# Two weight sums and one lo half of the FFN's fast product, made by adding DMA writes

## The chip, the cores and the metric

The kernel runs on one core of a Trainium2 chip. The engines of that core are TensorE (PE, with its weight loads PEld), VectorE (DVE), ScalarE (ACT), GpSimd (POOL) and SyncE (SP), which here only issues DMAs. The metric is the device time of one execution in microseconds (us). Before the change it is 2390.55 us, the median of three runs (2388.98 to 2391.84).

## The reference

One inference step of a 2-layer trunk for 512 prompt positions and 32 sample positions, which the kernel treats as 544 columns. All data is float32. Each layer has two gated feed-forward blocks (FFN) around a mixer and a memory attention:

```python
def _swiglu(x, wg, wu, wd):
    return (jax.nn.silu(x @ wg) * (x @ wu)) @ wd

x = x + 0.5 * _swiglu(_rmsnorm(x, n[0]), f1_wg[l], f1_wu[l], f1_wd[l])   # D_MODEL 1024, D_FF 2816
...
x = x + 0.5 * _swiglu(_rmsnorm(x, n[3]), f2_wg[l], f2_wu[l], f2_wd[l])
```

So there are four FFNs, f1 and f2 of either layer. The change is in the products `x @ wg` and `x @ wu`.

## The kernel before

**Split precision.** Every float32 operand is split in a hi half (a float32r copy, made by ACT) and a lo half (what is left, `source - hi`, made by VectorE). A product of two operands is three matmuls, hi·hi, hi·lo and lo·hi (`TERMS`, line 263). A weight tile is thus loaded raw, copied by ACT into `[:, 0]` and its remainder written by VectorE into `[:, 1]`.

**A fast 2x2 product.** For the gate and up projections a pair of 128-column blocks of the weights, both halves of the contraction and both halves of the columns of x are taken as 2x2 blocks, and a scheme with seven block products in place of eight is used. One such unit of work is called a pair, `P` (line 469). It reads 16 weight blocks of 128x128 per pair from `raw`, in four groups of four: blocks 0 to 3, 4 to 7, 8 to 11 and 12 to 15. Its weight operands are

- `al`: blocks 0 to 7 as they are (a12 and a11), used by products 2 and 1. `al_h` is the hi half (ACT), `al_l` the lo half (VectorE).
- `be`: two sums, `sb` = (blocks 4 to 7, blocks 8 to 11) each plus blocks 12 to 15 (`be_s`, VectorE), then hi (`be_h`, ACT) and lo (`be_l`, VectorE); products 7 and 5.
- `ga`: two further sums (`ga_s`, VectorE, into the tile `sg`), hi (`ga_h`) and lo (`ga_l`); products 6 and 3.
- `de`: blocks 8 to 11 as they are, `de_h` and `de_l`; product 4.

Each of the seven products is 12 matmuls of 272 columns (`prod`, line 390): four blocks of the contraction, and for each the three terms, the lo half of the weight being in the third.

**Order.** The order on every engine is the order in the program. For each FFN there are three parts: part 0 with 4 up pairs, after ordinary gate units (`gate`) have been computed for the same columns; part 1 with 8 pairs and part 2 with 6, gate and up in turn. That makes 18 pairs in an FFN and 72 in all. After each part a down projection (`dps`) follows. `run` (line 478) lays out seven steps for each pair: p1, p5, p4 of the pair before, p6, p2, p3, p7. Between them stands what the next pair, `N`, needs: `al_h` ahead of p4, `al_l` ahead of p6, `be_s` ahead of p2, `be_h` and `ga_s` ahead of p3, `be_l` and `ga_h` ahead of p7; `ga_l` stands ahead of the pair's own p1. The second pair of a part has no pair before it whose p4 is open when its `al_h` is made. The first pair of a part is prepared by `prelude` (line 474), one unit of TensorE work (48 matmuls) ahead of its p1.

**Loads and buffers.** Raw weights come in blocks of 1 MB through two buffers (`rawp`); `release` (line 153) issues the next block on SP when the last reader of a block is done, which for a pair is `de_l`. Split weights `al` and `be` take three buffers (`wcp`); `sb`, `sg`, `ga`, `de` and the hidden activations take 13 (`dp`). In the product stages POOL has no work.

Of the kernel before, what the change touches and what calls it, by code (L numbers as in the profile page):

```python
# [7 lines left out]
F32 = mybir.dt.float32  # L8
F32R = mybir.dt.float32r
AF = mybir.ActivationFunctionType  # L10
ALU = mybir.AluOpType
# [18 lines left out]
class Unit:  # L30
    def __init__(self, blk, k0, nk, c0, nc):
        self.blk, self.k0, self.nk, self.c0, self.nc = blk, k0, nk, c0, nc
        self.on_pool = self.late = self.raw = self.manual = False


class Block:
    def __init__(self, ap):
        self.ap = ap
        self.nk, self.nc = ap.shape[1], ap.shape[2]
        self.left = 0  # L40
        self.tile = None

    def unit(self, k0, nk, c0, nc):
        self.left += 1
# [4 lines left out]
def trunk_kernel(ctx, tc, I, O):  # L49
    nc = tc.nc  # L50
    pe, act, dve, pool, sp = nc.tensor, nc.scalar, nc.vector, nc.gpsimd, nc.sync
    keep = ctx.enter_context(tc.tile_pool(name="keep", bufs=1))
    up = ctx.enter_context(tc.tile_pool(name="up", bufs=49))
# [9 lines left out]
    def nm(s):  # L63
        cnt[0] += 1
        return f"{s}{cnt[0]}"
# [4 lines left out]
    def D(shape, dt=F32, n="d"):  # L70
        return dp.tile(shape, dt, tag="d", name=nm(n))
# [13 lines left out]
    def tt(e, out, a, b, op):  # L85
        e.tensor_tensor(out=out, in0=a, in1=b, op=op)  # L86
# [4 lines left out]
    def actv(out, a, f, **kw):  # L91
        act.activation(out=out, in_=a, func=f, **kw)  # L92
# [13 lines left out]
    def step(fn, *units, la=3, ahead=None):  # L106
        steps.append((fn, units, la, ahead))
# [7 lines left out]
    def flush():  # L115
        l, later[:] = list(later), []
        for f in l:
            f()
        for w in waiting:
            w[0] -= 1  # L120
        due = [w for w in waiting if w[0] <= 0]
        waiting[:] = [w for w in waiting if w[0] > 0]
        for w in due:
            w[1]()

    def emit_steps():
        order = []
        for _, us, _, _ in steps:
            order.extend(us)
        blks = []  # L130
        for u in order:
            if u.blk not in blks[-3:]:
                blks.append(u.blk)
        st = {"dma": 0, "conv": 0}

        def issue(part=0):
            if part:
                b = blks[0]
                h = b.nk // 2
                sp.dma_start(out=b.tile[:, h:], in_=b.ap[:, h:])  # L140
                return
            if st["dma"] >= len(blks):
                return
            b = blks[st["dma"]]
            st["dma"] += 1
            b.tile = rawp.tile([128, b.nk, b.nc], F32, tag="raw", name=nm("raw"))
            if st["dma"] == 1:
                h = b.nk // 2
                sp.dma_start(out=b.tile[:, 0:h], in_=b.ap[:, 0:h])
            else:  # L150
                sp.dma_start(out=b.tile, in_=b.ap)

        def release(u):
            u.blk.left -= 1
            if u.blk.left == 0:
                issue()

        def conv(defer=None):
            u = order[st["conv"]]
            st["conv"] += 1  # L160
            if u.manual:
                return
            w = wcp.tile([128, 2, u.nk, u.nc], F32R, tag="wc", name=nm("wc"))
            src = u.blk.tile[:, u.k0:u.k0 + u.nk, u.c0:u.c0 + u.nc]
            actv(w[:, 0], src, AF.Copy)
            u.tile = w

            def low():
                tt(pool if u.on_pool else dve, w[:, 1], src, w[:, 0].bitcast(F32), ALU.subtract)
                if not u.raw:  # L170
                    release(u)
            if defer is None or not u.late:
                low()
            else:
                defer.append(low)

        S["release"] = release
        startup(C_NORM, issue, conv)
        used = 0
        for fn, us, la, ahead in steps:  # L180
            used += len(us)
            flush()
            post = []
            while ahead is not None and st["conv"] < min(len(order), used + ahead):
                conv()
            while us and st["conv"] < min(len(order), used - len(us) + la):
                conv(post)
            fn(*us)
            for f in post:
                f()  # L190
            for u in us:
                if u.raw:
                    release(u)
        while later or waiting:
            flush()
# [95 lines left out]
    def ffn(which, l, next_g, tail=None):  # L291
# [53 lines left out]
        def low(lo, src, hi):  # L345
            tt(dve, lo, src, hi.bitcast(F32), ALU.subtract)

        def al_h(P):
            P.al = wcp.tile([128, 2, 8, 128], F32R, tag="wc", name=nm("wc"))
            actv(P.al[:, 0], P.blk.tile[:, 0:8], AF.Copy)  # L350

        def al_l(P):
            low(P.al[:, 1], P.blk.tile[:, 0:8], P.al[:, 0])

        def be_s(P):
            r = P.blk.tile.rearrange("p (z k) n -> p z (k n)", k=4)
            P.sb = D([128, 8, 128], n="sb")
            tt(dve, P.sb.rearrange("p (z k) n -> p z (k n)", k=4), r[:, 3:4].to_broadcast([128, 2, 512]), r[:, 1:3], ALU.add)

        def be_h(P):  # L360
            P.be = wcp.tile([128, 2, 8, 128], F32R, tag="wc", name=nm("wc"))
# [5 lines left out]

        def ga_s(P):
            r = P.blk.tile
            P.sg = D([128, 8, 128], n="sg")  # L370
            tt(dve, P.sg[:, 0:4], P.sb[:, 4:8], r[:, 4:8], ALU.add)
            tt(dve, P.sg[:, 4:8], P.sg[:, 0:4], r[:, 0:4], ALU.add)

        def ga_h(P):
            P.ga = D([128, 8, 128], F32R, n="ga"), D([128, 8, 128], F32R, n="ga")
            actv(P.ga[0], P.sg, AF.Copy)

        def ga_l(P):
            low(P.ga[1], P.sg, P.ga[0])
            P.sg = None  # L380

        def de_h(P):
            P.de = D([128, 2, 4, 128], F32R, n="de")
            actv(P.de[:, 0], P.blk.tile[:, 8:12], AF.Copy)

        def de_l(P):
            low(P.de[:, 1], P.blk.tile[:, 8:12], P.de[:, 0])
            S["release"](P)

        def prod(P, i, bank, first=False):  # L390
            w = {1: lambda p: P.al[:, p, 4:8], 2: lambda p: P.al[:, p, 0:4], 7: lambda p: P.be[:, p, 0:4], 5: lambda p: P.be[:, p, 4:8],
                 6: lambda p: P.ga[p][:, 0:4], 3: lambda p: P.ga[p][:, 4:8], 4: lambda p: P.de[:, p]}[i]
            for kp in range(4):
                for j, (p, xx) in enumerate(TERMS):
                    pe.matmul(out=bank[:, 0:HT], lhsT=w(p)[:, kp], rhs=XF[i, kp][xx], start=first and kp == 0 and j == 0,  # L395
                              stop=kp == 3 and j == 2, skip_group_check=not first)
# [24 lines left out]
        def p6(P):  # L421
            prod(P, 6, P.A)
            actv(P.s[:, 0], P.A[:, 0:HT], AF.Copy)

        def p2(P):
            B = PS("wB")
            prod(P, 2, B, True)
            P.al = None
            tt(dve, P.q[:, 0], B[:, 0:HT], P.q[:, 0], ALU.add)
            if P.up:  # L430
                g = G[P.p, 0]
                tt(dve, g[:, 0], P.q[:, 0], g[:, 0], ALU.mult)
                P.q = None
            else:
                actv(P.q[:, 0], P.q[:, 0], AF.Silu)
# [31 lines left out]
            P.A = None  # L467

        def pair(w, p, up):
            P = Block(w[p]).unit(0, 16, 0, 128)  # L470
            P.manual, P.up, P.p = True, up, p
            return P

        def prelude(P):
            for f in (al_h, be_s, ga_s, be_h, al_l, be_l, ga_h):
                f(P)

        def run(items):
            for i, P in enumerate(items):
                N = items[i + 1] if i + 1 < len(items) else None  # L480
                Q = items[i - 1] if i else None

                def nx(*fs, N=N):
                    for f in fs:
                        if N:
                            f(N)
                step(lambda _, P=P: (ga_l(P), p1(P)), P, la=1)
                step(lambda P=P: p5(P))
                step(lambda Q=Q, nx=nx: (nx(al_h), Q and p4(Q)), ahead=None if N else 1)
                step(lambda P=P, nx=nx: (de_h(P), nx(al_l), p6(P)))  # L490
                step(lambda P=P, nx=nx: (de_l(P), nx(be_s), p2(P)))
                step(lambda P=P, nx=nx: (nx(be_h, ga_s), p3(P)), ahead=None if N else 2)
                step(lambda P=P, nx=nx: (nx(be_l, ga_h), p7(P)))

        ks_of = lambda p0, np: [(k, 2 * p0 + k) for k in range(2 * np)]
        for part, (p0, np) in enumerate(((0, 4), (4, 4), (8, 3))):
            prs = range(p0, p0 + np)
            if part == 0:
                items = [pair(wu, p, True) for p in prs]
                for p in prs:  # L500
                    blk = Block(wg[p])
# [32 lines left out]
            for n2 in range(4):  # L534
                blk = Block(wd[n2])
                us += [blk.unit(0, 2 * np, i * 128, 128) for i in range(2)]
            a, b = ks[:-2], ks[-2:]
# [1485 lines left out]
```

## Time and profile before

| What | us |
|---|---|
| median of three runs | 2390.55 |
| lowest and highest of them | 2388.98, 2391.84 |
| the profiled execution | 2391.14 |
| its span | 2389.3 |
| its granted TensorE clock, mean | 0.996 of full |

The profile is of one execution. In its page "busy" is the time in which an engine had an instruction running; a group's row has the line, the engine, the tiles (out<-in), the count, then busy time and mean duration, then the idle time of the engine just before these instructions and what ended it. Most operations go through helpers (`tt` at line 86, `actv` at line 92, `mm` at line 95, the products at line 395), so the tiles' names tell them apart. The timeline has one row for each instruction or run of equal instructions: start and duration in us. A DMA's row has its size and the median time from issue to landing.

### The profile page before, as it was taken

Reading aid. Unit: us, or ns where it says so; the run is one execution under the profiler, and the core shown is the slowest. Engines: PE = TensorE matmul, PEld = TensorE weight load, DVE = VectorE, ACT = ScalarE, POOL = GpSimd, SP = SyncE. Lnnn points to the kernel's source line nnn. Section 1 sums busy time; section 2 is a strip of 40 time slices with the busy share of each in tenths; the row PEclk is TensorE's granted clock in tenths of the full one; section 3 lists DMA queues with packets and bytes.
Section 4 is the critical chain, followed back from the end, with each engine's and each line's share of the span. In section 5 each row is a group of like instructions: output and inputs, shape, how many; then the busy total and the mean of one; then the engine's idle time right before and its main releaser. Section 6 shows DMA issues by size and latency. Waiting matters only on the chain.

```text
span 2389.3 us, 46376 instructions
## 1 busy us (share of the span) xinstructions
PE 2349.7 (98%) x20030; PEld 2285.2 (96%) x20030; DVE 1570.2 (66%) x2443; ACT 1067.9 (45%) x1783; POOL 232.6 (10%) x243
## 2 busy tenths in 40 slices
PE   8999999998999999999999999999999999999998
PEld 8999999998889989999999999999999989999998
DVE  8758475668656655867666876747445656948484
ACT  6435255724545344534434543525443444525254
POOL 0000001244221103000000000000313002000001
PEclk9999999999999999999999999999999999999999
DMA  4222234223445471232322222322322552223222
GB/s 146 89 89 97 85 107 137 89 81 117 146 153 186 160 287 71 71 108 87 107 89 90 88 106 80 115 72 93 123 92 88 203 221 76 84 89 107 106 85 78
DMA packets 69197, 268.69 MB, mean 112 GB/s; under 512 B 15072, under 2 KB 22240, under 8 KB 45952
## 3 DMA queue, kind: packets, MB, share of 16 engines
q1 hardware_dynamic: 55264, 243.72, 29.1%
q10 hardware_dynamic: 13728, 22.01, 2.7%
q8 instruction: 157, 2.57, 0.4%
q14 instruction: 48, 0.39, 0.0%
HBM read 253.47 MB, written 12.23 MB: 111 GB/s over the span
## 4 chain that ended last, share of the span: by engine, by line
PE 86%; DVE 9%; ACT 2%; issue 1%; POOL 1%; DMA 0%; SPq 0%; ACTq 0%; DVEq 0%; POOLq 0%
PE dps L95 21%; PE wA L395 18%; PE wC L395 9%; PE wo L95 8%; PE wB L395 4%; PE vp L95 4%; PE q L95 4%; PE pA L95 2%; PE gps L95 2%; PE kp L95 2%; PE pB L95 2%; DVE wc L86 1%; DVE xf L86 1%; PE up L95 1%; PE sc L95 1%
## 5 line engine op out<-in xcount | busy, mean ns | idle before, releaser
L86 DVE TENSOR_TENSOR wc<-raw,wc 128x1024 fp32r<-128x1024 f32 (+1 forms) x306 | 381.9, 1253 | 250.5 <-ACT wc L92 249.6
L95 PE MATMUL dps<-hid,wc 128*128 128x272 f32 x4224 | 534.9, 288 | 0.6 <-DVE wc L86 0.6
L95 PEld LDWEIGHTS dps<-hid,wc 128*128 128x128 f32 x4224 | 531.5, 188 | 1.3 <-DVE wc L86 1.2
L92 ACT ACTIVATE wc<-raw 128x1024 fp32r<-128x1024 f32 (+1 forms) x322 | 331.0, 1032 | 249.9 <-PE dps L95 201.3
L89 DVE SCALAR_TENSOR_TENSOR x<-dps,x 128x272 f32<-128x272 f32 x192 | 75.7, 434 | 212.1 <-PE dps L95 212.1
L95 PE MATMUL gps<-xd,wc 128*128 128x272 f32 x1344 | 177.2, 291 | 7.5 <-ACT xd L92 6.8
L95 PEld LDWEIGHTS gps<-xd,wc 128*128 128x128 f32 x1344 | 172.8, 190 | 8.3 <-ACT xd L92 6.8
L86 POOL TENSOR_TENSOR ss<-ss,sq 128x544 f32<-128x544 f32 x47 | 65.4, 1392 | 1181.2 <-ACT sq L92 1172.5
L395 PE MATMUL wA<-xb,wc 128*128 128x272 f32 x864 | 122.2, 290 | 7.8 <-DVE wc L86 7.8
L92 ACT ACTIVATE wc<-sb 128x1024 fp32r<-128x1024 f32 x72 | 76.0, 1056 | 112.8 <-DVE sb L86 87.4
L395 PE MATMUL wC<-xf,wc 128*128 128x272 f32 x864 | 124.2, 292 | 0.4 <-DVE wc L86 0.4
L395 PEld LDWEIGHTS wA<-xb,wc 128*128 128x128 f32 x864 | 113.9, 190 | 8.9 <-DVE wc L86 8.7
L395 PE MATMUL wA<-xf,ga 128*128 128x272 f32 x864 | 120.3, 288 | 0.2
L395 PE MATMUL wA<-xf,wc 128*128 128x272 f32 x864 | 120.1, 288 | 0.0
L395 PE MATMUL wA<-xf,de 128*128 128x272 f32 x864 | 120.1, 288 | 0.0
L395 PE MATMUL wC<-xf,ga 128*128 128x272 f32 x864 | 120.0, 288 | 0.0
L395 PE MATMUL wB<-xf,wc 128*128 128x272 f32 x864 | 119.9, 288 | 0.0
L395 PEld LDWEIGHTS wC<-xf,wc 128*128 128x128 f32 x864 | 114.9, 190 | 2.7 <-DVE wc L86 1.3
L395 PEld LDWEIGHTS wA<-xf,ga 128*128 128x128 f32 x864 | 112.9, 188 | 0.9 <-ACT q L92 0.9
L395 PEld LDWEIGHTS wA<-xf,wc 128*128 128x128 f32 x864 | 112.9, 188 | 0.0
L395 PEld LDWEIGHTS wC<-xf,ga 128*128 128x128 f32 x864 | 112.9, 188 | 0.0
L395 PEld LDWEIGHTS wB<-xf,wc 128*128 128x128 f32 x864 | 112.8, 188 | 0.0
(366 smaller groups left out, 4428.0 us busy)
## 6 DMA issues: line engine op xcount, KB each, us to landing
raw<-in_f_wu_dram SPq DMA_DIRECT2D x44, 1024.0 KB, 4.7
raw<-in_f_wg_dram SPq DMA_DIRECT2D x43, 1024.0 KB, 4.8
raw<-in_f_wda_dram SPq DMA_DIRECT2D x16, 1024.0 KB, 4.8
raw<-in_f_wdb_dram SPq DMA_DIRECT2D x16, 1024.0 KB, 4.7
sk<-in_kcT_dram SPq DMA_DIRECT2D x32, 512.0 KB, 7.8
sv<-in_vc_dram SPq DMA_DIRECT2D x64, 256.0 KB, 7.1
raw<-in_w_in_even_dram SPq DMA_DIRECT2D x13, 1024.0 KB, 4.8
raw<-in_f_wdc_dram SPq DMA_DIRECT2D x16, 768.0 KB, 4.2
```

The lines of the kernel that those rows point to most:

```text
L86: e.tensor_tensor(out=out, in0=a, in1=b, op=op)
L89: dve.scalar_tensor_tensor(out=out, in0=a, scalar=s, in1=b, op0=op0, op1=op1)
L92: act.activation(out=out, in_=a, func=f, **kw)
L95: pe.matmul(out=out, lhsT=l, rhs=r, start=start, stop=stop)
L395: pe.matmul(out=bank[:, 0:HT], lhsT=w(p)[:, kp], rhs=XF[i, kp][xx], start=first and kp == 0 and j == 0, stop=kp == 3 and j == 2, skip_grou ...
```

## The change

The lo half of `al` and the two sums in `sb` are no longer made by VectorE.

- `al_l` goes. `al_h` also has ACT write the negated hi half into `al[:, 1]`, and POOL issues a DMA which adds blocks 0 to 7 from device memory onto it: source - hi. Both stand where `al_h` stood, ahead of p4.
- `be_s` goes. A pair's raw block is 12 blocks (768 KB) instead of 16. When it is issued, a hook (`extra`) also takes the buffer `sb`, has SP load blocks 12 to 15 into both of its halves (two DMAs of 256 KB), and has POOL issue a DMA which adds blocks 4 to 11 from device memory onto them (512 KB).
- `ga_s` writes its two sums into the raw buffer in place of a tile `sg` of its own; products 6 and 3 swap the halves that they read.

```diff
@@ emit_steps, issue @@
             b.tile = rawp.tile([128, b.nk, b.nc], F32, tag="raw", name=nm("raw"))
-            if st["dma"] == 1:
+            if b.extra:
+                sp.dma_start(out=b.tile, in_=b.ap)
+                b.extra(b)
+            elif st["dma"] == 1:
...
@@ ffn @@
         def al_h(P):
             P.al = wcp.tile([128, 2, 8, 128], F32R, tag="wc", name=nm("wc"))
             actv(P.al[:, 0], P.blk.tile[:, 0:8], AF.Copy)
-
-        def al_l(P):
-            low(P.al[:, 1], P.blk.tile[:, 0:8], P.al[:, 0])
-
-        def be_s(P):
-            r = P.blk.tile.rearrange("p (z k) n -> p z (k n)", k=4)
-            P.sb = D([128, 8, 128], n="sb")
-            tt(dve, P.sb.rearrange("p (z k) n -> p z (k n)", k=4), r[:, 3:4].to_broadcast([128, 2, 512]), r[:, 1:3], ALU.add)
+            actv(P.al[:, 1], P.al[:, 0].bitcast(F32), AF.Copy, scale=-1.0)
+            pool.dma_start(out=P.al[:, 1], in_=P.src[:, 0:8].bitcast(F32R), accum_op=ALU.add)
...
         def ga_s(P):
             r = P.blk.tile
-            P.sg = D([128, 8, 128], n="sg")
-            tt(dve, P.sg[:, 0:4], P.sb[:, 4:8], r[:, 4:8], ALU.add)
-            tt(dve, P.sg[:, 4:8], P.sg[:, 0:4], r[:, 0:4], ALU.add)
+            tt(dve, r[:, 4:8], P.sb[:, 4:8], r[:, 4:8], ALU.add)
+            tt(dve, r[:, 0:4], r[:, 4:8], r[:, 0:4], ALU.add)
...
         def pair(w, p, up):
-            P = Block(w[p]).unit(0, 16, 0, 128)
-            P.manual, P.up, P.p = True, up, p
+            src = w[p]
+            blk = Block(src[:, 0:12])
+            P = blk.unit(0, 12, 0, 128)
+            P.manual, P.up, P.p, P.src = True, up, p, src
+
+            def sums(b):
+                P.sb = D([128, 8, 128], n="sb")
+                for z in range(2):
+                    sp.dma_start(out=P.sb[:, 4 * z:4 * z + 4], in_=src[:, 12:16])
+                pool.dma_start(out=P.sb, in_=src[:, 4:12], accum_op=ALU.add)
+            blk.extra = sums
             return P
 
         def prelude(P):
-            for f in (al_h, be_s, ga_s, be_h, al_l, be_l, ga_h):
+            for f in (al_h, be_h, ga_s, be_l, ga_h):
                 f(P)
...
                 step(lambda Q=Q, nx=nx: (nx(al_h), Q and p4(Q)), ahead=None if N else 1)
-                step(lambda P=P, nx=nx: (de_h(P), nx(al_l), p6(P)))
-                step(lambda P=P, nx=nx: (de_l(P), nx(be_s), p2(P)))
+                step(lambda P=P, nx=nx: (de_h(P), p6(P)))
+                step(lambda P=P, nx=nx: (de_l(P), p2(P)))
                 step(lambda P=P, nx=nx: (nx(be_h, ga_s), p3(P)), ahead=None if N else 2)
```

More of the change, by code (lines that the diff above doesn't have):

```diff
@@ L40, in __init__ @@
         self.left = 0
-        self.tile = None
+        self.tile = self.extra = None
     def unit(self, k0, nk, c0, nc):
@@ L369, in ga_s @@
             r = P.blk.tile
-            P.sg = D([128, 8, 128], n="sg")
-            tt(dve, P.sg[:, 0:4], P.sb[:, 4:8], r[:, 4:8], ALU.add)
-            tt(dve, P.sg[:, 4:8], P.sg[:, 0:4], r[:, 0:4], ALU.add)
+            tt(dve, r[:, 4:8], P.sb[:, 4:8], r[:, 4:8], ALU.add)
+            tt(dve, r[:, 0:4], r[:, 4:8], r[:, 0:4], ALU.add)
         def ga_h(P):
             P.ga = D([128, 8, 128], F32R, n="ga"), D([128, 8, 128], F32R, n="ga")
-            actv(P.ga[0], P.sg, AF.Copy)
+            actv(P.ga[0], P.blk.tile[:, 0:8], AF.Copy)
         def ga_l(P):
-            low(P.ga[1], P.sg, P.ga[0])
-            P.sg = None
+            low(P.ga[1], P.blk.tile[:, 0:8], P.ga[0])
         def de_h(P):
@@ L391, in prod @@
             w = {1: lambda p: P.al[:, p, 4:8], 2: lambda p: P.al[:, p, 0:4], 7: lambda p: P.be[:, p, 0:4], 5: lambda p: P.be[:, p, 4:8],
-                 6: lambda p: P.ga[p][:, 0:4], 3: lambda p: P.ga[p][:, 4:8], 4: lambda p: P.de[:, p]}[i]
+                 6: lambda p: P.ga[p][:, 4:8], 3: lambda p: P.ga[p][:, 0:4], 4: lambda p: P.de[:, p]}[i]
             for kp in range(4):
```

## The prediction

> **What bounds the kernel now.** I read the page first: busy times, the clock, and the rows of the costly groups.
>
> ```profile
> span 2389.3 us, 46376 instructions
> PE 2349.7 (98%) x20030; PEld 2285.2 (96%) x20030; DVE 1570.2 (66%) x2443; ACT 1067.9 (45%) x1783; POOL 232.6 (10%) x243
> ...
> PEclk9999999999999999999999999999999999999999
> ...
> L395 PE MATMUL wA<-xb,wc 128*128 128x272 f32 x864 | 122.2, 290 | 7.8 <-DVE wc L86 7.8
> ...
> L395 PE MATMUL wA<-xf,ga 128*128 128x272 f32 x864 | 120.3, 288 | 0.2
> ...
> raw<-in_f_wu_dram SPq DMA_DIRECT2D x44, 1024.0 KB, 4.7
> ```
>
> TensorE is busy 98% at full clock; VectorE, which the change relieves, 66%. In the product stage the only wait worth a number is in front of p1 (`wA<-xb,wc`): 7.8 us in all, on a `wc` that VectorE writes. So that is about all that a faster VectorE can win there. The profiled execution took 2391.1 us (span 2389.3), 0.6 over the median of 2390.55; my sum starts from 2391.
>
> Next, the timeline of a steady pair of part 1 (first column start, second duration, us).
>
> ```profile
> 169.60 1.67 PE L395 MATMUL wA<-xf,de 128*128 128x272 f32 x12
> 170.10 1.05 ACT L92 ACTIVATE wc<-raw 128x1024 fp32r<-128x1024 f32 x1
> 171.18 1.22 DVE L86 TENSOR_TENSOR wc<-raw,wc 128x1024 fp32r<-128x1024 f32 x1 [1.52 <-ACT wc L92]
> ...
> 172.32 0.68 DVE L86 TENSOR_TENSOR de<-raw,de 128x512 fp32r<-128x512 f32 x1
> 172.93 1.22 DVE L86 TENSOR_TENSOR sb<-raw 128x1024 f32<-128x1024 f32 x1
> 173.03 0.33 SPq L151 DMA_DIRECT2D raw<-in_f_wu_dram  x1
> ...
> 174.38 1.06 ACT L92 ACTIVATE wc<-sb 128x1024 fp32r<-128x1024 f32 x1 [1.17 <-PE wB L395]
> ...
> 177.13 1.67 PE L395 MATMUL wA<-xb,wc 128*128 128x272 f32 x12
> 178.64 1.67 PE L395 MATMUL wC<-xf,wc 128*128 128x272 f32 x12
> 180.14 1.67 PE L395 MATMUL wA<-xf,de 128*128 128x272 f32 x12
> ```
>
> The period is 180.14 - 169.60 = 10.54 us, seven products of 1.5, with no gap: TensorE bounds it. The lo half of `al` is finished at 171.18 + 1.22 = 172.4, and p1 wants it with its third matmul, at 177.13 + 0.25 = 177.4: it lies ready 5 us. The change spends that reserve.
>
> **The change, part by part.** *Removed*: on VectorE, per pair, `al_l` (1.22) and `be_s` (1.22), over 72 pairs 2 x 88 = 176 us. In steady pairs that is worth nothing, since TensorE's matmuls cover it. It could count only where p1 waits: at the four starts of a part 0.
>
> ```profile
> 58.54 1.04 ACT L92 ACTIVATE wc<-raw 128x1024 fp32r<-128x1024 f32 x1
> ...
> 64.27 2.64 PE L395 MATMUL wA<-xb,wc 128*128 128x272 f32 x10 [4.11 <-DVE wc L86]
> ...
> 992.58 1.04 ACT L92 ACTIVATE wc<-raw 128x1024 fp32r<-128x1024 f32 x1
> ...
> 998.30 1.52 PE L395 MATMUL wA<-xb,wc 128*128 128x272 f32 x10 [1.25 <-DVE wc L86]
> ...
> 1366.28 1.05 ACT L92 ACTIVATE wc<-raw 128x1024 fp32r<-128x1024 f32 x1
> ...
> 1372.01 1.52 PE L395 MATMUL wA<-xb,wc 128*128 128x272 f32 x10 [1.21 <-DVE wc L86]
> ...
> 2047.33 1.05 ACT L92 ACTIVATE wc<-raw 128x1024 fp32r<-128x1024 f32 x1
> ...
> 2053.05 1.52 PE L395 MATMUL wA<-xb,wc 128*128 128x272 f32 x10 [1.27 <-DVE wc L86]
> ```
>
> Those waits are 4.11 + 1.25 + 1.21 + 1.27 = 7.84 us, the group's 7.8.
>
> *Added on ACT*: the negated copy, 72 x 1.05 = 76 us. ACT is at 45% and TensorE covers the work; but the copy stands in the chain of `al`, and the `de` copy behind it starts 1.05 later. So `de_l`, which releases the raw buffer, ends near 174.0 instead of 173.0, and the next raw load goes out then. P4, the user of `de`, comes at 180; nothing else is late.
>
> *Added on SP*: two loads of `sb` (256 KB each) behind a raw load that shrinks to 768 KB: 1.25 MB instead of 1, two more issues of 0.33. `P.sb` now takes its `dp` buffer a pair earlier, but `sg` no longer takes one; by the code no more than 13 are held, so I price that wait of SP at nothing. If it failed, SP's later raw loads would queue behind it.
>
> *Added on POOL*: two adding DMAs per pair. The sums' add waits on POOL for the two `sb` loads, and the `al` add of the following pair stands behind it in POOL's queue. POOL has no other work in these stages.
>
> *The term that decides* is the trip of the `al` add, D: from the end of the negated copy to TensorE's use. Against it stand these reserves, copy start + 2 x 1.05 up to p1's third matmul:
>
> ```profile
> 79.72 1.06 ACT L92 ACTIVATE wc<-raw 128x1024 fp32r<-128x1024 f32 x1
> ...
> 86.37 1.67 PE L395 MATMUL wA<-xb,wc 128*128 128x272 f32 x12
> ...
> 160.97 1.05 ACT L92 ACTIVATE wc<-raw 128x1024 fp32r<-128x1024 f32 x1
> ...
> 166.48 1.67 PE L395 MATMUL wA<-xb,wc 128*128 128x272 f32 x12
> ```
>
> - start of a part 0: 992.58 + 2.09 = 994.67 to 998.30: **3.63**; at the other three 3.64, 3.63, 3.62. Four pairs.
> - second pair of each part (no p4 stands between, as after 160.97): 163.07 to 166.73: **3.66**. Twelve pairs.
> - later pairs of part 0: 81.84 to 86.62: **4.78**. Two in each FFN, eight.
> - later pairs of parts 1 and 2: 172.20 to 177.38: **5.18**. Six and four in each FFN, forty.
> - The first pairs of parts 1 and 2 (eight) have their copy before the last `down` unit, with about 10 us, and cost nothing.
>
> A late add isn't caught up: the next `al` copy stands behind p5 on ACT, so the lateness is paid once in each pair.
>
> Before has no adding DMA and none from POOL, so D is bounded by other transfers:
>
> ```profile
> sk<-in_kcT_dram SPq DMA_DIRECT2D x32, 512.0 KB, 7.8
> ...
> xd<-x ACTq DMA_DIRECT2D x8, 272.0 KB, 2.1
> ...
> AT<-dA ACTq DMA_DIRECT2D x1, 512.0 KB, 3.4
> ```
>
> The add carries 512 KB. Below, a plain 512 KB took 3.4 (the shortest 272 KB, 2.1); above, 7.8 with queueing. The row I go by is the 1 MB raw load, since an add has to read its target as well and so handles 512 KB twice. The windows view of one such load (issued at 163.91; the last two figures are the DMA share and GB/s):
>
> ```profile
> 163.91:164.81 0.90, 0.90 (x9) 0.90 (x9) 0.90 (x1) 0.00 (x0) 0.00 (x0) 1.00 0.00 0
> 164.81:167.91 3.10, 3.10 (x27) 3.10 (x26) 3.07 (x6) 2.38 (x3) 0.00 (x0) 1.00 0.95 333
> 167.91:168.71 0.80, 0.80 (x7) 0.74 (x7) 0.80 (x3) 0.14 (x1) 0.00 (x0) 1.00 0.06 21
> ```
>
> So 0.9 us before data, 3.1 with all engines full, 0.8 to landing: 4.8 alone. But in every later pair the next raw load goes out at 174.04, 1.84 after the add (172.20), and its data flows from 2.74 on, when the add would need until 4.0: the shared 1.26 us take twice as long. I take **D = 6.0** there and at second pairs, and 4.8 at the four starts, where no raw load is issued into it.
>
> The Trainium skill (Collectives: The Full Stack, "The bandwidth ceiling") says that an add in the DMA datapath halves the rate because it needs two source reads; no run here shows it, and the sum by it is the one that follows.
>
> Sum: 4 x (4.8 - 3.63) = 4.7; 12 x (6.0 - 3.66) = 28.1; 8 x (6.0 - 4.78) = 9.8; 40 x (6.0 - 5.18) = 32.8; together 75 us. 2391 + 75 = **2466 us**, 3.1% slower.
>
> The sums' add is the next in line: raw and `sb` land near 181, the add 6 us later at 187; `be_h`, at 174.38 + 10.54 = 184.9 before, then waits, and ga_s (1.4) and be_l (1.22) behind it end about 189.6 for a p5 that wants be_l near 189.4. That is level, and a stretched pair gives it room; I count nothing.
>
> **The rivals.** *A, the add is about as quick as a plain write* (its reads overlap): D between 3.9 and 5, for example 4.4: 4 x 0.8 + 12 x 0.74 = 12 us, 2403. For it: the 3.4 row. Against it: the raw load that collides.
>
> The Trainium skill (DMA: Bandwidth & Descriptors, "Anatomy of one DMA — SWDGE (gpsimd) path") fits a GpSimd-issued DMA as 2.0 us + bytes/436e3; an estimate by it is 3.2 us for 512 KB, which would bring rival B.
>
> *B, hidden or faster*: D below 3.9. The place is the four starts; the price, what is left of 7.84 us. At D = 3.4 they win 4 x 0.23 = 1 us (2390, no change); from D = 2.4 on, where 1.2 is won at each, 5 us (2386, faster by 0.2%). Only the 272 KB row is that short.
>
> *C, the adds queue*: two adds of 3.1 us data and 3.9 for 1.25 MB fill 10.1 of a 10.54 us period. The `al` add then stands behind the sums' add, D = 7.8 as in the `sk` row, in the 48 later pairs: 4.7 + 28.1 + 8 x 3.02 + 40 x 2.62 = 162 us, 2553. Against it: a longer pair thins the traffic.
>
> *D, POOL's adds take much longer than any row* (descriptors made in software, 10 us or more): 48 x 5 us and more, over 2600.
>
> **How the numbers follow.** Forecast (D 5 to 7) 0.45; A 0.20; B 0.19, of it faster 0.06; C 0.12; D 0.04. 0.2% (5 us), about what a measurement of this kernel can tell from no change, gives faster 0.06, same 0.13, slower 0.81. The range goes from A's quick end (2394) to C (2555); it leaves out most of B and all of D. The forecast alone is 2415 to 2520.
>
> **What would show it.** Right: a wait of `wA<-xb,wc` on a DMA, about 0.8 us in later pairs and over 2 in second pairs; the pair's period near 11.4; the adds landing 5 to 6 us after issue; VectorE near 1394 us, ACT near 1144; the DMA share at twice its tenths in the product stages. Wrong: adds landing in under 4 us; or waits in front of p5 (`wC<-xf,wc`), by which the sums' add and not `al` would be late; or SP waiting on `dp` buffers.

## The result and the profile after

The changed kernel takes 2594.31 us, median of four runs (2585.09 to 2608.72), against 2390.09 for the kernel before: a ratio of 1.0855, 95% interval 1.083 to 1.0879. The forecast was 2466 with a range of 2394 to 2555, so the sign was right, the size was not, and the time lies outside the range.

The page of the profiled execution (span 2590.3 us) has these lines in the place of those shown of before:

```profile
span 2590.3 us, 46970 instructions
PE 2408.5 (93%) x20030; PEld 2334.2 (90%) x20030; DVE 1414.5 (55%) x2299; ACT 1145.6 (44%) x1855; POOL 357.5 (14%) x387
...
PEclk9899999999999999999999999999999999999999
...
L390 PE MATMUL wA<-xb,wc 128*128 128x272 f32 x864 | 160.9, 332 | 151.3 <-DMA wc<-in_f_wu_dram 98.4
...
L390 PE MATMUL wC<-xf,wc 128*128 128x272 f32 x864 | 144.2, 325 | 0.0
...
L390 PE MATMUL wA<-xf,ga 128*128 128x272 f32 x864 | 120.7, 289 | 0.0
...
raw<-in_f_wu_dram SPq DMA_DIRECT2D x44, 768.0 KB, 6.5
sb<-in_f_wu_dram SPq DMA_DIRECT2D x88, 256.0 KB, 6.9
sb<-in_f_wu_dram POOLq DMA_DIRECT2D x44, 512.0 KB, 5.4
wc<-in_f_wu_dram POOLq DMA_DIRECT2D x44, 512.0 KB, 5.8
```

The span grew by 201.0 us, and two numbers hold all of it. The idle time in front of p1 (`wA<-xb,wc`) went from 7.8 to 151.3, 143.5 more, and it now ends with the adding DMA into `wc`. TensorE's busy time went from 2349.7 to 2408.5, 58.8 more, for the same 20030 matmuls. The growth sits in p1 and in the product after it: p1's busy time went from 122.2 to 160.9 us, its mean from 290 to 332 ns, and p5 (`wC<-xf,wc`) now has 325, while p6 (`wA<-xf,ga`), further behind the wait, has 289 after 288. No wait has appeared in front of p5 or p6.

The second number is for the most part a matter of the clock. The mean granted clock fell from 0.996 to 0.972. At a half-speed gate, 2590.3 x (1 - 0.972) x 2 = 145 us of the span ran at half speed, against 2389.3 x 0.004 x 2 = 19 before. The windows view around the wait at the start of one part 0 shows how (the first columns are the window and its length, then busy time of PE, PEld, DVE, ACT and POOL, then granted clock, DMA share and GB/s):

```profile
1048.00:1049.80 1.80, 0.00 (x0) 0.00 (x0) 0.00 (x0) 0.00 (x0) 0.00 (x0) 1.00 1.00 198
1049.90:1053.30 3.40, 2.27 (x10) 2.27 (x11) 0.00 (x0) 0.00 (x0) 0.00 (x0) 0.50 0.14 27
1053.40:1056.70 3.30, 3.30 (x17) 3.30 (x16) 0.00 (x0) 0.67 (x2) 0.00 (x0) 0.50 0.00 0
1056.80:1060.00 3.20, 3.20 (x28) 3.20 (x27) 0.58 (x1) 3.17 (x6) 0.84 (x1) 1.00 0.02 5
```

TensorE waited 4.84 us until 1051.03. The clock had dropped to 0.50 by 1049.90 and stayed there for two windows of 3.4 us; in the second of them 17 matmuls were done where the next window did 28. So a wait of a few microseconds is paid again in the products behind it. By the trace's clock records, half speed lasted 144.4 us in all (19.8 before), and TensorE had matmuls running in 115.1 us of it (11.5 before). At half speed half of such time is lost, so the clock took (115.1 - 11.5) / 2 = 51.8 of the 58.8 us. The other 7.0 are not the clock; a wait also breaks a product in two, and in the next timeline the two parts are busy for 0.41 + 1.51 us, where twelve matmuls in one go take 1.67. The Trainium skill (TensorE: Matmul & The Clock Gate, "Part 1: The HAM clock gate") gives a free-running window of about 3.4 us after which the clock is halved or restored; the trace agrees: its half-speed stretches last 3.41, 6.83 or 10.24 us, but for the last, during which the span ends.

The timeline of two successive pairs shows the wait itself (start, duration, then the idle time before it and what ended it):

```profile
187.84 0.86 POOL L474 DMA_DIRECT2D sb<-in_f_wg_dram  x1 [8.16 <-DMA sb<-in_f_wg_dram]
188.54 1.06 ACT L92 ACTIVATE wc<-wc 128x1024 fp32r<-128x1024 f32 x1
189.90 0.86 POOL L355 DMA_DIRECT2D wc<-in_f_wg_dram  x1 [1.19 <-ACT wc L92]
191.16 0.33 SPq L148 DMA_DIRECT2D raw<-in_f_wu_dram  x1
...
198.33 1.51 PE L390 MATMUL wA<-xb,wc 128*128 128x272 f32 x10 [3.44 <-DMA wc<-in_f_wg_dram]
...
200.47 0.86 POOL L474 DMA_DIRECT2D sb<-in_f_wu_dram  x1 [9.71 <-DMA sb<-in_f_wu_dram]
...
202.77 1.06 ACT L92 ACTIVATE wc<-wc 128x1024 fp32r<-128x1024 f32 x1
204.12 0.86 POOL L355 DMA_DIRECT2D wc<-in_f_wu_dram  x1 [2.78 <-ACT wc L92]
...
208.71 0.41 PE L390 MATMUL wA<-xb,wc 128*128 128x272 f32 x2
209.85 1.51 PE L390 MATMUL wA<-xb,wc 128*128 128x272 f32 x10 [0.73 <-DMA wc<-in_f_wu_dram]
```

In the first pair the negated copy ends at 188.54 + 1.06 = 189.60 and p1 goes on at 198.33: a trip of 8.73 us. The sums' add was issued 2.06 us before the `al` add. In the second pair the two adds are 3.65 us apart, and the trip from 203.83 to 209.85 is 6.02. Long and short waits follow each other like this through the product stages; the period of the later pairs in parts 1 and 2 is 13.9 us on the mean (10.8 to 18.7), where 11.4 had been forecast.

The trip goes by the distance between the two adds. Of the 64 `al` adds of the table below, 29 went out less than 3 us behind a sums' add: their trips are 8.48 us on the mean (6.28 to 10.88). The trips of the other 35 are 6.04 on the mean (5.42 to 10.69).

From the trace I took the trip of every `al` add, from the end of the negated copy to landing:

| Pairs | forecast | after, mean (min to max) | `al` add alone (first experiment), mean |
|---|---|---|---|
| starts of part 0 (4) | 4.8 | 7.40 (7.14 to 7.53) | 5.74 |
| second pairs (12) | 6.0 | 6.02 (5.42 to 7.45) | 6.09 |
| later, part 0 (8) | 6.0 | 7.54 (5.59 to 10.88) | 5.75 |
| later, parts 1 and 2 (40) | 6.0 | 7.38 (5.50 to 10.70) | 6.05 |

The starts and the later pairs are the ones that the forecast missed. The prediction's own sum with the measured trips is 4 x 3.77 + 12 x 2.36 + 8 x 2.76 + 40 x 2.20 = 153.5 us, against the 143.5 more that p1 waits. The model (trip less reserve, once per pair) holds; its trips did not, and a term for the clock was missing.

### The profile page after: what moved, and what is told of

It is laid out like the page before. It is cut to its first block, busy times and chain, and to the rows that moved or that the text cites. A ratio compares the mean times of both kernels' runs of the same rounds, so it can differ in the third digit from the quotient of the medians.

```text
span 2590.3 us, 46970 instructions
## 1 busy us (share of the span) xinstructions
PE 2408.5 (93%) x20030; PEld 2334.2 (90%) x20030; DVE 1414.5 (55%) x2299; ACT 1145.6 (44%) x1855; POOL 357.5 (14%) x387
## 3 DMA queue, kind: packets, MB, share of 16 engines
q0 software_dynamic: 20736, 75.51, 17.1%
## 4 chain that ended last, share of the span: by engine, by line
PE 68%; DMA 18%; ACT 6%; DVE 5%; issue 2%; POOL 1%; SPq 0%; ACTq 0%; POOLq 0%; DVEq 0%
PE dps L95 20%; DMA wc<-in_f_wu_dram 10%; PE wA L390 8%; PE wo L95 7%; PE wC L390 6%; DMA wc<-in_f_wg_dram 5%; PE gps L95 5%; ACT wc L92 4%; PE vp L95 4%; PE q L95 4%; PE pA L95 2%; PE kp L95 2%; DMA sb<-in_f_wu_dram 2%; PE pB L95 1%; PE up L95 1%
## 5 line engine op out<-in xcount | busy, mean ns | idle before, releaser
L86 DVE TENSOR_TENSOR wc<-raw,wc 128x1024 fp32r<-128x1024 f32 (+1 forms) x234 | 293.2, 1260 | 208.3 <-ACT wc L92 207.4
L390 PE MATMUL wA<-xb,wc 128*128 128x272 f32 x864 | 160.9, 332 | 151.3 <-DMA wc<-in_f_wu_dram 98.4
L390 PEld LDWEIGHTS wA<-xb,wc 128*128 128x128 f32 x864 | 137.2, 222 | 165.4 <-DMA wc<-in_f_wu_dram 107.9
L86 DVE TENSOR_TENSOR de<-raw,de 128x512 fp32r<-128x512 f32 x72 | 49.6, 688 | 217.3 <-ACT de L92 217.3
L390 PE MATMUL wC<-xf,wc 128*128 128x272 f32 x864 | 144.2, 325 | 0.0
L390 PEld LDWEIGHTS wC<-xf,wc 128*128 128x128 f32 x864 | 138.0, 228 | 0.0
L390 PEld LDWEIGHTS wA<-xf,de 128*128 128x128 f32 x864 | 116.5, 194 | 0.0
```

## The experiments

What makes the trip long? Theory Q: the sums' add, issued on the same POOL queue shortly before. Theory R: SP's raw load, which uses the same DMA engines at the same time. Theory S: an adding DMA is slow in itself, whatever stands ahead. The `al` add and the sums' add were first run apart. Times are medians, ratios are to the kernel before, with their 95% interval.

**1. The `al` add alone.** The kernel before, with only the part of the change that concerns `al`; VectorE still forms `be_s`, and raw blocks stay 1 MB.

```diff
         def al_h(P):
...
-            low(P.al[:, 1], P.blk.tile[:, 0:8], P.al[:, 0])
+            actv(P.al[:, 1], P.al[:, 0].bitcast(F32), AF.Copy, scale=-1.0)
+            pool.dma_start(out=P.al[:, 1], in_=P.src[:, 0:8].bitcast(F32R), accum_op=ALU.add)
```

> Only the al add is left (the sums are VectorE's again, raw blocks 1 MB). Theory Q, the al add is late because the sums' add stands ahead of it in POOL's queue: every al add now takes 5.4 to 5.8 us from the end of the negated copy, so later pairs wait 0.3 us (40) or 0.8 (8), second pairs 1.9 (12), starts of part 0 1.9 (4): 50 us of waits, few half-clock stretches, about 2445 us. Theory R, it is late because it shares the DMA engines with SP's raw load: that load is still 1 MB and stands at the same place, so trips stay between 5.5 and 10 us and the time near 2560. Theory S, the adding itself is slow: like R, above 2500.

2495.18 us, 1.044 (1.0417 to 1.0463). The page:

```profile
PE 2388.6 (95%) x20030; PEld 2313.7 (92%) x20030; DVE 1490.4 (60%) x2371; ACT 1143.3 (46%) x1855; POOL 292.9 (12%) x315
...
L394 PE MATMUL wA<-xb,wc 128*128 128x272 f32 x864 | 148.0, 312 | 82.9 <-DMA wc<-in_f_wu_dram 61.2
...
raw<-in_f_wu_dram SPq DMA_DIRECT2D x44, 1024.0 KB, 6.7
...
wc<-in_f_wu_dram POOLq DMA_DIRECT2D x44, 512.0 KB, 5.5
```

The trips (last column of the table) are those of an add with nothing before it in its queue: 5.74 at the starts, where no raw load runs beside it, and 5.75 (part 0) and 6.05 (parts 1 and 2) in later pairs, where one does. The median is 5.8 in all three groups; the higher mean comes from three trips over 6.6 us, of which one reaches 9.5, and what lengthened those isn't settled. So the collision costs the add 0.3 us at most, not 1.26, and theory R fails; the raw load pays, landing in 6.7 us instead of 4.7. With these trips the prediction's sum gives 4 x 2.11 + 12 x 2.43 + 8 x 0.97 + 40 x 0.87 = 80 us, and p1 waits 82.9 - 7.8 = 75 more. TensorE's busy time rose by 38.9, of which the clock, counted as above, is 29.5. (Together that is 114 us in the profiled execution, which at 2504.78 us was the longest of the four.) Q was right that the trip falls, but its 2445 us was missed: trips and waits came out higher than its 5.4 to 5.8 and 50 us, and the half-speed stretches were not few. The time alone would not tell Q from S; the trips do.

**2. The sums' add alone.** The changed kernel, with `al_l` back on VectorE.

```diff
-            actv(P.al[:, 1], P.al[:, 0].bitcast(F32), AF.Copy, scale=-1.0)
-            pool.dma_start(out=P.al[:, 1], in_=P.src[:, 0:8].bitcast(F32R), accum_op=ALU.add)
+
+        def al_l(P):
+            low(P.al[:, 1], P.blk.tile[:, 0:8], P.al[:, 0])
...
-            for f in (al_h, be_h, ga_s, be_l, ga_h):
+            for f in (al_h, al_l, be_h, ga_s, be_l, ga_h):
...
-                step(lambda P=P, nx=nx: (de_h(P), p6(P)))
+                step(lambda P=P, nx=nx: (de_h(P), nx(al_l), p6(P)))
```

> Only the sums' add is left (the lo half of al is VectorE's again, early in the prelude). Theory Q and theory R: no wait of TensorE on a DMA in front of p1; the sums' add lands 5.4 us after issue, in time, and the four starts of part 0 lose VectorE's waits, so 2380 to 2392 us. Theory S: the sums' add would still be late for be, with waits in front of p5, above 2420 us.

2384.8 us, 0.9973 (0.9963 to 0.9983): 0.3% faster than the kernel before, and as Q and R expected.

```profile
PE 2347.2 (98%) x20030; PEld 2284.2 (96%) x20030; DVE 1494.6 (63%) x2371; ACT 1071.3 (45%) x1783; POOL 294.9 (12%) x315
...
L391 PE MATMUL wC<-xf,wc 128*128 128x272 f32 x864 | 121.2, 288 | 4.3 <-DVE wc L86 4.0
L391 PE MATMUL wA<-xb,wc 128*128 128x272 f32 x864 | 120.7, 289 | 1.5 <-DVE wc L86 1.5
L391 PE MATMUL wA<-xf,ga 128*128 128x272 f32 x864 | 120.6, 288 | 1.6 <-ACT q L92 1.6
...
sb<-in_f_wu_dram POOLq DMA_DIRECT2D x44, 512.0 KB, 5.4
```

The same kind of add, landing in the same 5.4 us, costs nothing here, because its reader comes later than that. The wait in front of p1 falls from 7.8 to 1.5, since `al_l` no longer queues behind `be_s` in the prelude. Whether moving `al_l` forward there would give the same without any adding DMA was not run. Alone, the parts give +104 and -6 us, which together would be +98; the whole change gives +204. The other 106 arise only where both adds are there.

**3. Plain writes.** The changed kernel, with both POOL DMAs writing in place of adding; `al`'s lo half and the sums are then not formed (the second half of `al` holds the blocks themselves, `sb` holds blocks 4 to 11).

```diff
-            pool.dma_start(out=P.al[:, 1], in_=P.src[:, 0:8].bitcast(F32R), accum_op=ALU.add)
+            pool.dma_start(out=P.al[:, 1], in_=P.src[:, 0:8].bitcast(F32R))
...
-                pool.dma_start(out=P.sb, in_=src[:, 4:12], accum_op=ALU.add)
+                pool.dma_start(out=P.sb, in_=src[:, 4:12])
```

> Both POOL DMAs write plainly instead of adding, so the lo half of al and the sums are replaced by the bare weights (that part of the computation is left out); order, sizes and waits are the same. Theory S: a plain write lands 1.5 us sooner or more, 4 us or less after issue, most waits go, 2430 us or less. Theories Q and R: the trip alone stays within 1 us of the add's 5.4, the alternation of short and long waits remains, and the time stays above 2520 us.

2464.61 us, 1.0315 (1.0295 to 1.0335).

```profile
PE 2372.8 (96%) x20030; PEld 2301.7 (93%) x20030; DVE 1412.0 (57%) x2299; ACT 1143.4 (46%) x1855; POOL 309.0 (13%) x387
...
L390 PE MATMUL wA<-xb,wc 128*128 128x272 f32 x864 | 140.8, 307 | 59.7 <-DMA wc<-in_f_wu_dram 34.7
...
sb<-in_f_wu_dram POOLq DMA_DIRECT2D x44, 512.0 KB, 3.8
wc<-in_f_wu_dram POOLq DMA_DIRECT2D x44, 512.0 KB, 4.5
```

The row of POOL's DMA queue (packets, MB, share of 16 engines' span), of the changed kernel and then of this run:

```profile
q0 software_dynamic: 20736, 75.51, 17.1%
```

```profile
q0 software_dynamic: 20736, 75.51, 10.1%
```

The same 512 KB into `sb` land in 3.8 us when written and 5.4 when added: 1.6 us, or 42%, more. On POOL itself a DMA got cheaper as well: its busy time fell by 357.5 - 309.0 = 48.5 us over 144 of them, 0.34 of the 0.86 that the timeline above shows for one. The Trainium skill (Collectives: The Full Stack, "The bandwidth ceiling") says that an add halves the rate. The trip of this one, with its fixed parts, is 1.4 times as long, but for the same bytes its packets hold the DMA engines for 17.1% of 2590.3 = 443 us instead of 10.1% of 2463.0 = 249, 1.8 times as long, which is close to that. The time lies between the two expectations, above 2430 and below 2520, so both bounds were missed and both theories have a share: adding itself is worth 2594 - 2465 = 130 of the 204 us, and 74 remain with writes that don't add. Writes still follow each other closely on POOL's queue, and the trips in the later pairs of part 0 still go from 3.73 to 9.68.

**4. The sums' add right behind the `al` add.** If POOL's queue is what counts, exchanging the two must move the delay from `al` to the sums.

```diff
             pool.dma_start(out=P.al[:, 1], in_=P.src[:, 0:8].bitcast(F32R), accum_op=ALU.add)
+            pool.dma_start(out=P.sb, in_=P.src[:, 4:12], accum_op=ALU.add)
...
-                pool.dma_start(out=P.sb, in_=src[:, 4:12], accum_op=ALU.add)
```

> The sums' add is issued behind the al add of the same pair instead of ahead of the al add of the pair before. Theory Q: al trips of 5.4 to 6 us everywhere, p1 waits near 0.5 us in later pairs and 2 in the 16 others, some 55 us in all; be may now be late by up to 1 us in front of p5; 2440 to 2480 us. Theory R: al trips unchanged, 5.5 to 10 us, above 2550.

2982.89 us, 1.248 (1.2449 to 1.2512). The page and the waits:

```profile
L391 PE MATMUL wC<-xf,wc 128*128 128x272 f32 x864 | 235.2, 438 | 349.2 <-ACT wc L92 290.4
...
L391 PE MATMUL wA<-xb,wc 128*128 128x272 f32 x864 | 139.8, 309 | 48.8 <-DMA wc<-in_f_wu_dram 45.3
...
wc<-in_f_wu_dram POOLq DMA_DIRECT2D x44, 512.0 KB, 5.4
sb<-in_f_wu_dram POOLq DMA_DIRECT2D x44, 512.0 KB, 10.2
```

The delay moved as Q has it: the `al` add now lands in 5.4 us, p1 waits 48.8, and the sums' add takes 10.2 and makes p5 wait 349.2. Two adds of 512 KB issued together land 5 and 10 us later; whichever stands second pays for both. SP still issues the raw load and two `sb` loads per pair here, so these loads are not what makes the `al` add late in the changed kernel. The time itself was missed by 500 us: p5 was to wait up to 1 us per pair and waits 349.2 / 72 = 4.9, for the sums' add now goes out later as well as behind another. The clock falls to 0.901 and TensorE's busy time rises to 2545.1.

**5 and 6. More reserve.** `al`'s copies and add are issued ahead of p5 rather than ahead of p4, in the `al`-only kernel (5) and in the whole change (6).

```diff
-                step(lambda P=P: p5(P))
-                step(lambda Q=Q, nx=nx: (nx(al_h), Q and p4(Q)), ahead=None if N else 1)
+                step(lambda P=P, nx=nx: (nx(al_h), p5(P)))
+                step(lambda Q=Q, nx=nx: (Q and p4(Q),), ahead=None if N else 1)
```

> The al add alone, as in e1_al_only, but the al copy, its negation and the add stand ahead of p5 instead of p4: 1.5 us more reserve in every pair but the first of a part. Theory, the wait is trip minus reserve: trips of 5.4 to 6 us against 6.2 to 6.7 leave later pairs no wait, second pairs (5.2) about 0.5, the four starts 3.4 as before; some 20 us over the kernel before with the half-clock stretches, 2400 to 2425 us. Rival, the al copy then waits for its raw load (which landed 6.1 to 6.7 us after issue there) and the reserve doesn't grow: as e1_al_only, 2480 us or more.

> The whole change, with the al add ahead of p5. Theory Q (the al add stands behind the sums' add in POOL's queue when that was issued less than 3 us ahead): the al add now comes about when the sums' add does, so trips of 7 to 10 us remain in part of the pairs, against reserves of 5.2 and 6.7; 2430 to 2530 us. Rival, only the trip of a lone add counts: as e5_al_only_early, 2425 us or less.

Measured: 2440.59 us, 1.0209 (1.0195 to 1.0223), and 2548.5 us, 1.0668 (1.0651 to 1.0684). Group rows of 5, then of 6:

```profile
L394 PE MATMUL wA<-xb,wc 128*128 128x272 f32 x864 | 136.2, 299 | 43.0 <-DMA wc<-in_f_wu_dram 31.9
```

```profile
L390 PE MATMUL wA<-xb,wc 128*128 128x272 f32 x864 | 154.5, 328 | 113.7 <-DMA wc<-in_f_wu_dram 57.0
```

Issuing a product (1.5 us) earlier takes 40 us from p1's wait in 5 and 38 in 6, so the lateness is what is paid. In 5 more had been expected (2425 us at most): the moved copy now stands behind other ACT work and at times waits for its raw block (23.5 us in 20 waits on gate weights, in the waits view), so the reserve grew by less than a product. In 6, where the time is 18 us above the range expected, the mean trip in the later pairs of parts 1 and 2 is 7.85 us, longer than in the change as it was: the sums' add is still ahead, and earlier copies don't get away from it.

**7. A gain on experiment 2's kernel?** That kernel (the sums' add alone), with `be_l` ahead of `ga_s` in the prelude (`be_l0` is `be_l` without the release of `sb`, which `sb_end` does).

```diff
-            for f in (al_h, al_l, be_h, ga_s, be_l, ga_h):
+            for f in (al_h, al_l, be_h, be_l0, ga_s, sb_end, ga_h):
```

> The sums' add alone, as in e2_sums_only, with be_l ahead of ga_s in the prelude. The waits of p5 on be at the four starts (4.0 us in all) go; 2378 to 2384 us, 0.3 to 0.5% under the kernel before. Rival: ga_h and ga_l come later by 1.2 us and p6 waits in its place, 2384 us or more.

2387.94 us, 0.9989 (0.9981 to 0.9998): no gain on experiment 2's 2384.8, and outside the 2378 to 2384 expected.

```profile
L391 PE MATMUL wA<-xf,ga 128*128 128x272 f32 x864 | 121.4, 290 | 4.4 <-ACT q L92 4.4
...
L391 PE MATMUL wC<-xf,wc 128*128 128x272 f32 x864 | 120.4, 288 | 1.7 <-DVE wc L86 1.7
```

P5's wait falls from 4.0 to 1.7, and p6's rises from 1.6 to 4.4: the wait only changes its place.

**8. The negated copy alone.** The kernel before, with ACT writing the negated half, which `al_l` then overwrites. The prediction had this copy at nothing.

```diff
             actv(P.al[:, 0], P.blk.tile[:, 0:8], AF.Copy)
+            actv(P.al[:, 1], P.al[:, 0].bitcast(F32), AF.Copy, scale=-1.0)
```

> The kernel before with the negated copy on ACT added (VectorE's al_l then overwrites it): what the change adds on ACT, alone. Theory: TensorE's work covers it and the later release of the raw buffer; the four starts may grow by up to 1.05 us each; 2390 to 2396 us. Rival, ACT's chain is part of the loss: 2410 us or more.

2429.43 us, 1.0163 (1.0148 to 1.0178): 39 us, unexpected. One line of the waits and three of the timeline:

```profile
PE wC L396 <- DVE wc L86: 26.9, 40, 1.3
```

```profile
167.21 1.23 DVE L86 TENSOR_TENSOR wc<-raw,wc 128x1024 fp32r<-128x1024 f32 x1 [3.68 <-ACT wc L92]
...
172.11 1.22 DVE L86 TENSOR_TENSOR wc<-sb,wc 128x1024 fp32r<-128x1024 f32 x1
173.38 1.53 PE L396 MATMUL wC<-xf,wc 128*128 128x272 f32 x10 [0.87 <-DVE wc L86]
```

VectorE waits 3.68 us for the copy, as `al_l` must follow it here; `de_l`, `be_s`, `ga_s` and `be_l` queue behind `al_l`, `be_l` ends at 173.33, and p5 goes on at 173.38: it waits for `be_l` in 40 pairs. The 40 waits are 26.5 us more than before; the rest of the loss is TensorE's busy time, 13.5 us more for 40 broken products, of which the clock is only 2.7. TensorE and ACT at 45% were no cover, for VectorE's chain behind the copy had no slack of 1.05 us. In the changed kernel p5's idle time is 0.0; there neither `al_l` nor `be_s` stands on VectorE. That this is why the copy costs nothing there is a reading of these rows: no run took the copy alone out of the change.

**9 and 10. The `al` add in two halves,** the one that p1 reads first in front, in the `al`-only kernel (9) and in the whole change (10).

```diff
-            pool.dma_start(out=P.al[:, 1], in_=P.src[:, 0:8].bitcast(F32R), accum_op=ALU.add)
+            for k in (4, 0):
+                pool.dma_start(out=P.al[:, 1, k:k + 4], in_=P.src[:, k:k + 4].bitcast(F32R), accum_op=ALU.add)
```

> The al add alone, cut in two of 256 KB, the half that p1 reads first. Theory, trip minus reserve, with a trip that has a fixed part and a part by size (POOL's 0.9, and about half of the 4.3 behind it): the first half arrives 4.0 to 4.4 us after the negated copy, later pairs (4.8 and 5.2) don't wait, second pairs and starts wait 0.4 to 0.8; 2396 to 2410 us. Rival, the trip doesn't go by size: as e1_al_only, about 2495 us.

> The whole change with the al add cut in two, the half of p1 first. Theory Q: the half still stands behind the sums' add in POOL's queue, so trips of 4 us where that was issued 3 us ahead or more and of 6 to 8 us elsewhere; 2450 to 2520 us. Rival, the queue doesn't matter and only size and reserve do: as e9_al_only_split, 2410 us or less.

2492.09 us, 1.0432 (1.0415 to 1.0449), and 2603.7 us, 1.0889 (1.0873 to 1.0905): no gain in either, where both had been expected to gain. Rows of 9:

```profile
L395 PE MATMUL wA<-xb,wc 128*128 128x272 f32 x864 | 136.6, 297 | 42.2 <-DMA wc<-in_f_wu_dram 33.8
...
L395 PE MATMUL wC<-xf,wc 128*128 128x272 f32 x864 | 134.8, 297 | 19.8 <-DVE wc L86 19.6
...
raw<-in_f_wu_dram SPq DMA_DIRECT2D x44, 1024.0 KB, 7.9
```

And its waits view:

```profile
ACT wc L92 <- DMA raw<-in_f_wu_dram: 47.3, 27, 2.6
...
ACT wc L92 <- DMA raw<-in_f_wg_dram: 25.4, 18, 2.1
```

P1 waits 42.2 instead of 82.9, and its half does come sooner, 4.1 us after the copy in later pairs, as expected. But the raw load slows once more, from 6.7 to 7.9 us, ACT waits 47.3 and 25.4 us for raw blocks, and p5 waits for `be_l` again, as in 8, though `al_l` is gone here. TensorE's busy time stays at 2385.4, 35.7 above the kernel before, although half speed lasts only 30.9 us: 111 waits in the product stages, nearly all under 1 us, break products, where the kernel before has 5. So most of the gain in front of p1 is given back behind it. In 10 p1 still waits 152.0 us, as in the unsplit change: where the sums' add went out less than 3 us ahead, the first half's trip is 9.0 us on the mean, and elsewhere 4.4. What stands ahead in the queue is not shortened by halving what follows.

## Why the prediction missed

**What held.** TensorE bounds, and a late `al` add is paid in front of p1, once per pair, as trip less reserve: with measured trips the sum gives 153.5 for 143.5 measured (80 for 75 in experiment 1). VectorE's total is 1414.5 (1394 forecast), ACT's 1145.6 (1144). A lone add lands 5.4 to 5.5 us after issue, within the 5 to 6 forecast. The DMA share of the product stage doubled as forecast: the windows view has 0.28 before and 0.58 after, from 120 to 240 us. No wait appeared in front of p5, and SP waited only 4.0 us in all (nine waits) ahead of its `sb` loads.

**The step that failed: D, the trip of the `al` add.** The sum took D = 4.8 at the starts and 6.0 elsewhere, from the 1 MB load and its collision with the next raw load; the sums' add that stands ahead in POOL's queue had no part in it. Measured, D is 7.40 at the starts and 7.54 and 7.38 in the later pairs, so the four terms of the sum are 15.1, 28.3, 22.1 and 88.0 us in place of 4.7, 28.1, 9.8 and 32.8. The second pairs' term came out right by luck: 6.0 was put together as 4.8 alone and 1.26 of collision, and alone it is 5.7 and the collision 0.3 at most, two errors that cancelled. "I count nothing" was said of the sums' add being late for p5, and that held; what the same add does to the `al` add was given no term.

What the sum left out stood in the prediction's own text: the `al` add stands behind a sums' add in POOL's queue. The longer trips are that, by the distances in the changed kernel (8.48 us close behind it, 6.04 elsewhere), by experiment 1 (without it the trip falls to 5.7 to 6.1) and by experiment 4 (exchanged, the delay moves to the sums). It was rival C, "the adds queue", with D = 7.8 and 0.12. Its waits, 162 us, are near those measured, but as a mean: it had 7.8 in every later pair and 4.8 at the starts, and the trips of the later pairs go from 5.50 to 10.88. It was held unlikely because "a longer pair thins the traffic". That reads the queue as a matter of bandwidth over a period. Both adds hang on the pair's progress: in the timeline the sums' add goes out 2.06 and 3.65 us ahead of the `al` add although a pair lasts over 11 us, and thinner traffic doesn't part them.

**The missing term: the clock.** No term stood for what happens after a wait. It is 58.8 us, 29% of the loss (51.8 of them half speed, the rest not), and puts the time outside the range: C's 2553 with it would have been 2612.

**The starts.** 4.8 was taken for want of a colliding raw load. They measure 5.74 without the sums' add and 7.40 with it, for one stands ahead there as well, that of the second pair. The timeline of the start whose clock was shown:

```profile
1043.15 0.87 POOL L474 DMA_DIRECT2D sb<-in_f_wu_dram  x1 [13.26 <-DVE xf L86]
...
1044.14 0.86 POOL L355 DMA_DIRECT2D wc<-in_f_wu_dram  x1
...
1051.03 2.64 PE L390 MATMUL wA<-xb,wc 128*128 128x272 f32 x10 [4.84 <-DMA wc<-in_f_wu_dram]
```

The adds are 0.99 us apart, and the second comes 6.9 us after its issue.

**The ACT copy.** "Nothing else is late" is right for the changed kernel (p5 idle 0.0) and wrong for the copy by itself on the kernel before (experiment 8, 39 us). The forecast looked at ACT's share and not at the VectorE chain behind the copy, nor at the relief that goes with the change there.

**Whether adding is the cost.** "About as quick as a plain write" (rival A) is excluded: 5.4 against 3.8 us. A's time, 2403, does not come with plain writes either: they take 2465, with trips that still reach 9.68.

## What to carry to other kernels

Before moving work to an adding DMA, set its trip from issue to landing (here 5.4 us for 512 KB) against the time until its reader: the sums' add had that time and cost nothing, the `al` add had 3.6 to 5.2 us and its kernel lost 4.4%. Two such DMAs that hang on the same progress meet in one queue again and again (29 times of 64 here), and the second pays for the first, although the queue's packets take only 17% of the engines' time. Price each wait of a bound TensorE twice: the wait, and what it does to the products behind it (here 58.8 us behind 143.5 of added waits).

## What the runs showed of the hardware

- An adding DMA of 512 KB from POOL lands in 5.4 us, a writing one in 3.8; with another add issued just before it, 10.2.
- Beside a POOL add, the load on SP's queue pays more than the add: 1 MB lands in 6.7 us instead of 4.7, and the add is 0.3 us longer at most. The add had been issued 0.6 to 1.7 us before the load, so whether the order or the queue decides isn't shown. The Trainium skill (DMA: Bandwidth & Descriptors, "SWDGE vs HWDGE vs iDMA") says that a DMA engine takes turns between the two kinds of queue; taking turns alone does not say why the load loses so much more, and no run here tests it.
- Half-speed stretches come in pieces of 3.4 us and reach well into work that is already running: in the windows shown, products ran at half speed from 1051.03 to 1056.7, 5.7 us after a wait of 4.84.
- Of TensorE's waits in the product stages of the changed kernel, none of the 31 under 2 us had a half-speed stretch begin in it or within 3.5 us of its end; 12 of the 15 between 2 and 4 us and all 15 above 4 us had. In experiment 1, 4 of the 11 between 1 and 2 us had one too.
